# Four accumulating DMA transfers from GpSimd in place of three VectorE sums per weight block of a down projection, and PSUM banks that change roles between its two halves

## The chip, the core and the metric

The kernel runs on one core of a Trainium2 chip. A core has five engines with a program each: TensorE (PE, matrix products, with its weight loads listed apart as PEld), VectorE (DVE), ScalarE (ACT), GpSimd (POOL) and SyncE (SP, which here issues transfers). They run side by side and wait for each other by semaphores; on each engine instructions run in the order in which they are written down. The metric is device time in microseconds, the median of several executions.

## What is computed

The reference is one decoder layer for 256 tokens of width 2048. The change lies in its last matrix product.

```python
D_MODEL = 2048
D_FF = ((8 * D_MODEL // 3 + 255) // 256) * 256      # 5632
...
        x = x + rmsnorm(mix, post_mix_norm[l])

        hf = rmsnorm(x, pre_ffn_norm[l])
        ff = (jax.nn.silu(hf @ w_gate[l]) * (hf @ w_up[l])) @ w_down[l]
        x = x + rmsnorm(ff, post_ffn_norm[l])
```

`w_down` is the matrix of 5632 x 2048 that the last product reads.

## The kernel before

Every float32 weight block goes through four stations. SP loads 1 MB into one of four stage buffers (`st`, 128 partitions x 2048 values). ACT makes the float16 high part (`whi`, line 99), DVE the float16 rest (`wlo`, line 100); both write into rings of eight buffers. PE multiplies: three matmuls per product (high by high, high by low, low by high).

The down projection comes last. It has two units `u` (the left and the right 1024 output columns). A unit reads 22 blocks `i`, each 256 rows of `w_down` by 1024 columns, held in `st` as four sub-blocks of 128 rows by 512 columns. Ten of the 22 (`FAST`: 0, 2, ... 18) use a scheme with 7 products in place of 8 (21 matmuls instead of 24); it needs, beside three of the sub-blocks, four sums of sub-blocks. Blocks run in the order fast, plain, fast, plain, ...; the last three of a unit are plain and are called the tail.

For a fast block `load_pair` does this, in this order: split A (high and low parts of the first three sub-blocks, 1536 columns), the sums, in place in `st` (lines 730 to 732), split B (high and low parts of the four sums, 2048 columns). A plain block has one split of 2048 columns, called S here. The first two products of a fast block and one more use split A, the other four split B. In a regular stretch ACT and DVE therefore run B, S, A of the next fast block, then the sums on DVE, B, S, A, and so on.

PSUM has eight banks, four named `acc` and four named `tmp`. In a unit, `E` (four banks, one per half of the tokens and of the columns) and `X`, `Y`, `Z`, `Q` (four more) collect the products. When the last fast block is done, `X` to `Q` are combined by one ACT copy and four DVE operations into `fix`; the tail goes into `E`; `down_out` adds the two. Before the change `E` is always `acc` and `X` to `Q` are always `tmp`.

While the last blocks of the gate and up projections (j = 20 and 21) are still being multiplied, the first down blocks are already loaded and split; the ACT and DVE operations of `swiglu` (lines 640, 645, 99, 100) stand among these splits. A tile scheduler sets the order on each engine from the program's order.

Of the kernel before, what the change touches and what calls it, by code (L numbers as in the profile page):

```python
# [14 lines left out]
ALU = mybir.AluOpType  # L15
AX = mybir.AxisListType

P = 128
# [33 lines left out]
def hymba_layer(ctx: ExitStack, tc: tile.TileContext, x, xT, pos, inv_freq, g_pre, w_in, w_lat,  # L52
                q_norm, w_uqn, w_uqp, kv_norm, w_uk, w_uv, conv_w, conv_v, g_attn,
                w_out, g_post, g_ffn, w_gu, w_dn, g_ffo, out):
    nc = tc.nc
# [28 lines left out]
    def nm(base):  # L84
        uid[0] += 1
        return f"{base}_{uid[0]}"

    def acc_tile():
        return ps_acc.tile([P, 512], F32, tag="acc", name=nm("acc"))

    def tmp_tile():
        return ps_tmp.tile([P, 512], F32, tag="tmp", name=nm("tmp"))
# [198 lines left out]
    for j in range(4):  # L291
# [6 lines left out]
        for tb in range(NTB):  # L298
# [4 lines left out]
            u = work.tile([P, 256], F32, tag="C", name=nm("u"), bufs=2)  # L303
# [322 lines left out]
    def a_of(k, tb):  # L626
        return aT[:, k // 2, 4 * tb + k % 2, :], aT[:, k // 2, 4 * tb + 2 + k % 2, :]

    def fast_of(j):

        s = FAST.index(j)
        return ([(aT[:, j, b, :], aT[:, j, 4 + b, :]) for b in range(4)]
                + [(sT[:, s, b, :], sT[:, s, 3 + b, :]) for b in range(3)])
# [50 lines left out]
    def down_out(tb, j, ps, f):  # L684
        cs = slice(j * 512, (j + 1) * 512)
        nc.vector.tensor_tensor(f, ps, f, op=ALU.add)
        nc.scalar.activation(junk_tile(512), f, AF.Square, scale=UD, accum_out=ssd[:, tb, j : j + 1])
        if j == 3:
            final_scale(tb)
        nc.vector.scalar_tensor_tensor(ffg[:, tb, cs], f, UD, g_fo[:, cs], op0=ALU.mult, op1=ALU.mult)  # L690
# [4 lines left out]
    def partial_scale(tb):  # L695
        t = smalls()
        nc.vector.tensor_reduce(t, ssd[:, tb, 0:3], axis=AX.X, op=ALU.add)
        nc.vector.tensor_scalar(t, t, 1.0 / D, EPS, op0=ALU.mult, op1=ALU.add)
        ss_part[tb] = t
# [8 lines left out]
    def final(tb):  # L708
        r = r_fin[tb]
        cuts = (0, 640, 1280, 1792, 2048)  # L710
        for j in range(4):
            cs = slice(cuts[j], cuts[j + 1])
            xs = x_back[tb][:, cs]
            nc.vector.scalar_tensor_tensor(xs, ffg[:, tb, cs], r, xs, op0=ALU.mult, op1=ALU.add)
            (nc.sync if j % 2 == 0 else nc.scalar).dma_start(out[tb * P : (tb + 1) * P, cs], xs)

    def parts_of(st, n):
        hi = wsp.tile([P, 2048], F16, tag="whi", name=nm("whi"))
        lo = wsp.tile([P, 2048], F16, tag="wlo", name=nm("wlo"))
        split(hi[:, :n], lo[:, :n], st.rearrange("p b n -> p (b n)")[:, :n], WD_S)  # L720
        return [(hi[:, c : c + 512], lo[:, c : c + 512]) for c in range(0, n, 512)]

    def load_pair(u, i):

        st = stage.tile([P, 2048], F32, tag="stage", name=nm("st")).rearrange("p (b n) -> p b n", b=4)
        nc.sync.dma_start(st, w_dn[u, i])
        if i not in FAST:
            return parts_of(st, 2048)
        parts = parts_of(st, 1536)
        nc.vector.tensor_tensor(st[:, 0:4:3, :], st[:, 0:2, :], st[:, 3:4, :].to_broadcast([P, 2, 512]), op=ALU.add)  # L730
        nc.vector.tensor_tensor(st[:, 1, :], st[:, 0, :], st[:, 1, :], op=ALU.add)
        nc.vector.tensor_tensor(st[:, 2, :], st[:, 1, :], st[:, 2, :], op=ALU.add)
        return parts + parts_of(st, 2048)


# [2 lines left out]
    TAIL = 3  # L738
    x_back = {}
    for u in range(2):  # L740
        E = [[acc_tile(), acc_tile()], [acc_tile(), acc_tile()]]
        X, Y, Z, Q = [tmp_tile() for _ in range(4)]
        begun = set()

        def mm(ps, key, a, b, last=False):

            (ah, al), (bh, bl) = a, b
            nc.tensor.matmul(ps, ah, bh, start=key not in begun, stop=False)  # L748
            nc.tensor.matmul(ps, ah, bl, start=False, stop=False)  # L749
            nc.tensor.matmul(ps, al, bh, start=False, stop=last)  # L750
            begun.add(key)

        def plain(i, w, tb, c, last=False):

            mm(E[tb][c], (tb, c), a_of(2 * i, tb), w[0 if c == 0 else 3])
            mm(E[tb][c], (tb, c), a_of(2 * i + 1, tb), w[2 if c == 0 else 1], last)

        lasts = {f: FAST[-1] == f for f in FAST}
        for n, i in enumerate(order[:-TAIL]):
            w = load_pair(u, i)  # L760
            if i not in FAST:
                for tb in range(NTB):
                    for c in range(2):
                        plain(i, w, tb, c)
                continue
            A22, A11, A12, S1, S3, S2, S4 = fast_of(i)
            end = lasts[i]
            mm(E[0][0], (0, 0), A12, w[2])
            mm(E[0][1], (0, 1), S4, w[1])
            mm(X, "X", A11, w[0], end)  # L770
            mm(Y, "Y", S2, w[4], end)
            mm(Z, "Z", S3, w[6], end)
            mm(Q, "Q", S1, w[3], end)
            mm(E[1][0], (1, 0), A22, w[5])


        xs_ = work.tile([P, 512], F32, tag="hl", name=nm("xs"))
        nc.scalar.copy(xs_, X)
        m = work.tile([P, 512], F32, tag="ss", name=nm("m"), bufs=3)
        nc.vector.tensor_tensor(m, xs_, Y, op=ALU.subtract)  # L780
        n_ = work.tile([P, 512], F32, tag="ss", name=nm("n"), bufs=3)
        nc.vector.tensor_tensor(n_, m, Z, op=ALU.add)
        q2 = work.tile([P, 512], F32, tag="ss", name=nm("q2"), bufs=3)
        nc.vector.tensor_tensor(m, Q, m, op=ALU.subtract)
        nc.vector.tensor_tensor(q2, Q, n_, op=ALU.subtract)
        fix = [[xs_, m], [n_, q2]]
        tail = [(i, load_pair(u, i)) for i in order[-TAIL:]]
        if u == 1:
            for tb in range(NTB):
                x_back[tb] = stage.tile([P, 2048], F32, tag="stage", name=nm("xb"))  # L790
                nc.sync.dma_start(x_back[tb], x_off[:, tb, :])
        i, w = tail[0]
        for tb in range(NTB):
            for c in range(2):
                plain(i, w, tb, c)
        for tb in range(NTB):
            for c in range(2):
                for i, w in tail[1:]:
                    plain(i, w, tb, c, i == order[-1])
                down_out(tb, 2 * u + c, E[tb][c], fix[tb][c])  # L800
                if u == 1 and c == 0:
                    partial_scale(tb)
            if u == 1:
                final(tb)
# [80 lines left out]
```

## Time and profile before

| | us |
|---|---|
| median of 3 runs | 1015.67 (1015.43 to 1017.02) |
| the profiled execution | 1016.03 |
| its span in the trace | 1014.2 |
| PE busy in the span | 975.7 |
| DVE busy | 742.5 |
| ACT busy | 532.5 |
| POOL busy | 37.7 |

The span runs from the first to the last traced instruction; 1.83 us of the profiled execution lie around it. PE busy is counted from pipelined matmuls whose ends are modelled, so a full PE is one that always has a matmul in flight. The down projection fills the last 230 us of the span.

### The profile page before, as it was taken

The page shows a single profiled execution, that of the slowest core. Times are in us where ns is not written, and L with a number is a line of the kernel's source. Part 1 is how long each engine was busy: PE and PEld are TensorE (multiplying, and loading weights), DVE is VectorE, ACT ScalarE, POOL GpSimd, SP SyncE. Part 2 cuts the span into 40 slices and gives each one's busy share as a digit, 9 for nine tenths or more (in the row PEclk, how much of TensorE's full clock was granted, in tenths as well). Part 3 has the DMA queues.
Part 4 walks back from the last instruction along what each step waited for, and adds up shares of the span by engine and source line. Part 5 has one row for each costly group of instructions (what it writes and reads, how often), then busy time and mean ns, then how long its engine had stood idle before and what let it go on. Part 6 is the DMA issues. An engine that isn't in the chain of part 4 may idle for free.

```text
span 1014.2 us, 11941 instructions
## 1 busy us (share of the span) xinstructions
PE 975.7 (96%) x4652; PEld 462.3 (46%) x4652; DVE 742.5 (73%) x860; ACT 532.5 (53%) x599; POOL 37.7 (4%) x50
## 2 busy tenths in 40 slices
PE   6999997999999999999999999999999999989996
PEld 2444553774444444444444444444444444434442
DVE  6699999999868886555455555555556788888787
ACT  7796665664746564454444444454443544554551
POOL 0000000034100100000000000000000000000000
PEclk9999998999999999999999999999999999999998
DMA  9874666576546998676766776777755555635453
GB/s 348 330 256 140 223 209 196 166 241 222 201 166 170 321 303 290 218 228 201 240 217 206 222 224 223 226 218 217 234 198 166 176 189 224 235 127 222 166 186 145
DMA packets 77769, 220.37 MB, mean 217 GB/s; under 512 B 49552, under 2 KB 50192, under 8 KB 55184
## 3 DMA queue, kind: packets, MB, share of 16 engines
q1 hardware_dynamic: 76992, 218.68, 64.2%
q10 hardware_dynamic: 720, 0.93, 0.3%
q8 instruction: 36, 0.59, 0.2%
q14 instruction: 21, 0.17, 0.1%
HBM read 204.25 MB, written 4.19 MB: 206 GB/s over the span
## 4 chain that ended last, share of the span: by engine, by line
PE 64%; DVE 18%; issue 5%; ACT 5%; POOL 2%; DMA 1%; DVEq 0%; POOLq 0%; ACTq 0%; SPq 0%
PE acc L146 16%; PE acc L145 16%; PE acc L144 16%; DVE wlo L100 7%; DVE arena L277 3%; PE acc L749 3%; PE acc L750 3%; PE acc L748 3%; ACT whi L99 3%; DVE st L730 1%; PE tmp L749 1%; PE tmp L750 1%; PE tmp L748 1%; POOL sm L198 1%; DVE arena L285 1%
## 5 line engine op out<-in xcount | busy, mean ns | idle before, releaser
L100 DVE SCALAR_TENSOR_TENSOR wlo<-st,whi 128x2048 f16<-128x2048 f32 (+4 forms) x211 | 451.7, 2157 | 203.3 <-ACT whi L99 203.3
L99 ACT ACTIVATE whi<-st 128x2048 f16<-128x2048 f32 (+4 forms) x211 | 376.2, 1800 | 320.7 <-PE acc L146 176.5
L144 PE MATMUL acc<-whi,arena 128*128 128x512 f16 (+1 forms) x1084 | 410.1, 378 | 5.5 <-ACT whi L99 5.5
L145 PE MATMUL acc<-wlo,arena 128*128 128x512 f16 (+1 forms) x1084 | 410.4, 379 | 3.9 <-DVE wlo L100 3.8
L146 PE MATMUL acc<-whi,arena 128*128 128x512 f16 (+1 forms) x1084 | 409.8, 378 | 0.0
L144 PEld LDWEIGHTS <-arena 128*128 128x128 f16 x1084 | 106.7, 98 | 130.2 <-ACT arena L104 4.9
L146 PEld LDWEIGHTS <-arena 128*128 128x128 f16 x1084 | 106.7, 98 | 129.6 <-issue 6.9
L145 PEld LDWEIGHTS <-arena 128*128 128x128 f16 x1084 | 106.5, 98 | 125.2 <-issue 2.5
L748 PE MATMUL acc<-whi,arena 128*128 128x512 f16 x232 | 87.9, 379 | 0.0
L749 PE MATMUL acc<-wlo,arena 128*128 128x512 f16 x232 | 87.9, 379 | 0.0
L750 PE MATMUL acc<-whi,arena 128*128 128x512 f16 x232 | 87.9, 379 | 0.0
L277 DVE SCALAR_TENSOR_TENSOR arena<-arena 128x256 f32<-128x256 f32 x184 | 78.0, 480 | 0.0
L640 ACT ACTIVATE sg<-acc,r_f 128x256 f32<-128x256 f32 x44 | 20.7, 473 | 58.8 <-PE acc L146 58.8
L749 PEld LDWEIGHTS <-arena 128*128 128x128 f16 x272 | 26.6, 98 | 32.3 <-issue 0.3
L748 PEld LDWEIGHTS <-arena 128*128 128x128 f16 x272 | 26.6, 98 | 32.1
L750 PEld LDWEIGHTS <-arena 128*128 128x128 f16 x272 | 26.6, 98 | 32.1
L283 ACT ACTIVATE x_sb<-arena 128x256 f32<-128x256 f32 x56 | 25.2, 506 | 11.7 <-DVE arena L285 11.7
L705 POOL TENSOR_TENSOR sm<-sm,neg_half 128x1 f32<-128x1 f32 x2 | 1.1, 541 | 657.0 <-DVE sm L703 657.0
L730 DVE TENSOR_TENSOR st<-st 128x1024 f32<-128x1024 f32 x20 | 24.5, 1224 | 0.6
L153 PE MATMUL tmp<-arena,whi 128*128 128x256 f16 x80 | 21.8, 273 | 0.0
L154 PE MATMUL tmp<-arena,whi 128*128 128x256 f16 x80 | 21.8, 273 | 0.0
L155 PE MATMUL tmp<-arena,wlo 128*128 128x256 f16 x80 | 21.8, 273 | 0.0
(186 smaller groups left out, 610.1 us busy)
## 6 DMA issues: line engine op xcount, KB each, us to landing
st<-in_w_gu SPq DMA_DIRECT2D x88, 1024.0 KB, 5.0
st<-in_w_dn SPq DMA_DIRECT2D x44, 1024.0 KB, 4.9
st<-in_w_out SPq DMA_DIRECT2D x16, 1024.0 KB, 5.1
st<-in_w_in SPq DMA_DIRECT2D x14, 1024.0 KB, 9.3
st<-in_w_lat SPq DMA_DIRECT2D x12, 896.0 KB, 5.0
x_sb<-in_x SPq DMA_DIRECT2D x4, 1024.0 KB, 8.7
st<-in_w_uqn SPq DMA_DIRECT2D x4, 768.0 KB, 4.9
st<-in_w_uv SPq DMA_DIRECT2D x2, 1024.0 KB, 6.0
```

Of the source, the lines that this page charges most:

```text
L99: nc.scalar.activation(hi, src, AF.Copy, scale=scale)
L100: nc.vector.scalar_tensor_tensor(lo, src, scale, hi, op0=ALU.mult, op1=ALU.subtract)
L144: nc.tensor.matmul(p_ap, xh, wh, start=(start and k == 0), stop=False)
L145: nc.tensor.matmul(p_ap, xh, wl, start=False, stop=False)
L146: nc.tensor.matmul(p_ap, xl, wh, start=False, stop=(stop and k == wgt.kt - 1))
L153: nc.tensor.matmul(ps, wh[:, c0 : c0 + P], xh, start=(k == 0), stop=False)
L277: nc.vector.scalar_tensor_tensor(cacc[:, cb, :], upad[:, cb, k : k + S], cw[:, cb, k : k + 1], cacc[:, cb, :], op0=ALU.mult, op1=ALU.add)
L283: nc.scalar.activation(t[:, i, :], upad[:, cb, k : k + S], AF.Copy, scale=cw[:, cb, k : k + 1])
L730: nc.vector.tensor_tensor(st[:, 0:4:3, :], st[:, 0:2, :], st[:, 3:4, :].to_broadcast([P, 2, 512]), op=ALU.add)
L748: nc.tensor.matmul(ps, ah, bh, start=key not in begun, stop=False)
L749: nc.tensor.matmul(ps, ah, bl, start=False, stop=False)
L750: nc.tensor.matmul(ps, al, bh, start=False, stop=last)
```

## The change

The three DVE additions become four transfers issued by GpSimd. Each reads one sub-block of `st`, adds it to another sub-block of the same `st`, and writes it there: 128 partitions x 512 float32, 256 KB. They run in the sequence 0 += 3, 3 += 1, 1 += 0, 2 += 1, which gives the same four sums. Beside that, in unit 1 `E` takes the `tmp` banks and `X` to `Q` the `acc` banks.

```diff
         parts = parts_of(st, 1536)
-        nc.vector.tensor_tensor(st[:, 0:4:3, :], st[:, 0:2, :], st[:, 3:4, :].to_broadcast([P, 2, 512]), op=ALU.add)
-        nc.vector.tensor_tensor(st[:, 1, :], st[:, 0, :], st[:, 1, :], op=ALU.add)
-        nc.vector.tensor_tensor(st[:, 2, :], st[:, 1, :], st[:, 2, :], op=ALU.add)
+
+        for d, p in ((0, 3), (3, 1), (1, 0), (2, 1)):
+            nc.gpsimd.dma_start(st[:, d, :], st[:, p, :], accum_op=ALU.add)
         return parts + parts_of(st, 2048)
...
     for u in range(2):
-        E = [[acc_tile(), acc_tile()], [acc_tile(), acc_tile()]]
-        X, Y, Z, Q = [tmp_tile() for _ in range(4)]
+
+        mine, other = (acc_tile, tmp_tile) if u == 0 else (tmp_tile, acc_tile)
+        E = [[mine(), mine()], [mine(), mine()]]
+        X, Y, Z, Q = [other() for _ in range(4)]
```

GpSimd's order in the middle of unit 0, after the change; `st_6186` and `st_6251` are two fast blocks, a DMASW semaphore counts a transfer that GpSimd issued, a DMAHW semaphore one from SP.

```order
L732 DMA st_6186<-st_6186 128x512 [waits DMAHW7_49,DMASW7_49,DVE_49]
L732 DMA st_6186<-st_6186 128x512 [waits DMASW4_49]
L732 DMA st_6186<-st_6186 128x512 [waits DMASW5_49]
L732 DMA st_6186<-st_6186 128x512 [waits DMASW6_49]
L732 DMA st_6251<-st_6251 128x512 [waits DMAHW3_49,DMASW3_49,DVE_49]
L732 DMA st_6251<-st_6251 128x512 [waits DMASW0_49]
```

The first transfer of a block waits for DVE (split A); each of the others waits for the transfer ahead of it. In the kernel before GpSimd has nothing here.

DVE's order in the same place, before the change: split S of a plain block, split A of a fast block (`st_6247`), its sums, its split B, the next S.

```order
L100 SCALAR_TENSOR_TENSOR wlo_6220<-st_6217,whi_6219 128x2048 [waits DMAHW0_49,Activation_49]
L100 SCALAR_TENSOR_TENSOR wlo_6250<-st_6247,whi_6249 128x1536 [waits DMAHW1_49,Activation_49]
L730 TENSOR_TENSOR st_6247<-st_6247 128x2x512 [waits DVE_49]
L731 TENSOR_TENSOR st_6247<-st_6247 128x512 [waits DVE_49]
L732 TENSOR_TENSOR st_6247<-st_6247 128x512 [waits DVE_49]
L100 SCALAR_TENSOR_TENSOR wlo_6257<-st_6247,whi_6256 128x2048 [waits Activation_49]
L100 SCALAR_TENSOR_TENSOR wlo_6284<-st_6281,whi_6283 128x2048 [waits DMAHW4_49,Activation_49]
```

The same place after the change, where the fast block is `st_6251`:

```order
L100 SCALAR_TENSOR_TENSOR wlo_6224<-st_6221,whi_6223 128x2048 [waits DMAHW0_49,Activation_49]
L100 SCALAR_TENSOR_TENSOR wlo_6254<-st_6251,whi_6253 128x1536 [waits DMAHW3_49,Activation_49]
L100 SCALAR_TENSOR_TENSOR wlo_6262<-st_6251,whi_6261 128x2048 [waits DMASW2_49,DMASW1_49,DMASW3_49,DMASW0_49,Activation_49]
L100 SCALAR_TENSOR_TENSOR wlo_6289<-st_6286,whi_6288 128x2048 [waits DMAHW4_49,Activation_49]
L100 SCALAR_TENSOR_TENSOR wlo_6319<-st_6316,whi_6318 128x1536 [waits DMAHW5_49,Activation_49]
```

The sums are gone from DVE, the order of the splits is the same, and split B waits for the block's four transfers.

ACT's order there after the change: B of `st_6251`, S of the plain block, A of the next fast block `st_6316`, its B.

```order
L99 ACTIVATE whi_6261<-st_6251 128x2048 [waits DMASW1_49,DMASW0_49,DMASW2_49,DVE_49,DMASW3_49,PE_49,Activation_49]
L99 ACTIVATE whi_6288<-st_6286 128x2048 [waits DVE_49,DMAHW4_49,PE_49,Activation_49]
L99 ACTIVATE whi_6318<-st_6316 128x1536 [waits DMAHW5_49,DVE_49,PE_49]
L99 ACTIVATE whi_6326<-st_6316 128x2048 [waits DMASW5_49,DMASW6_49,DMASW4_49,DMASW7_49,DVE_49,PE_49]
```

Before the change the order of these four on ACT was the same, with a wait for DVE's sums where the DMASW semaphores stand now.

## Rows read from the trace of the kernel before

**Rows 1.** The profile's page: span, and busy time of each engine.

```profile
span 1014.2 us, 11941 instructions
PE 975.7 (96%) x4652; PEld 462.3 (46%) x4652; DVE 742.5 (73%) x860; ACT 532.5 (53%) x599; POOL 37.7 (4%) x50
```

**Rows 2.** Windows, 820 to 860 us: busy time per engine, clock, DMA share, GB/s.

```profile
820.00:860.00 40.00, 40.00 (x187) 18.20 (x186) 32.91 (x22) 18.97 (x12) 0.00 (x0) 1.00 0.50 187
```

**Rows 3.** Waits from 790 us on: who waited for whom, total, times, longest.

```profile
ACT whi L99 <- DVE st L732: 98.8, 17, 7.5
...
PE acc L748 <- DVE m L686: 3.2, 1, 3.2
...
PE tmp L749 <- DVE wlo L100: 1.1, 1, 1.1
```

**Rows 4.** Timelines of ACT and DVE, one regular period: start, duration, instruction, wait.

```profile
927.10 5.08 ACT L99 ACTIVATE whi<-st 128x2048 f16<-128x2048 f32 x3 [5.83 <-DVE st L732]
...
938.04 3.71 ACT L99 ACTIVATE whi<-st 128x2048 f16<-128x2048 f32 x2 [5.85 <-DVE st L732]
...
929.05 6.16 DVE L100 SCALAR_TENSOR_TENSOR wlo<-st,whi 128x2048 f16<-128x2048 f32 x3 [2.04 <-ACT whi L99]
935.24 1.22 DVE L730 TENSOR_TENSOR st<-st 128x1024 f32<-128x1024 f32 x1
```

**Rows 5.** Groups by line and shape, 795 to 1014 us: busy, mean ns, idle.

```profile
L100 DVE SCALAR_TENSOR_TENSOR wlo<-st,whi 128x2048 f16<-128x2048 f32 x38 | 85.3, 2288 | 33.6 <-ACT whi L99 33.6
...
L99 ACT ACTIVATE whi<-st 128x2048 f16<-128x2048 f32 x38 | 70.4, 1901 | 98.8 <-DVE st L732 98.8
```

**Rows 6.** DMA issues: count, KB each, median us from issue to landing.

```profile
st<-in_w_dn SPq DMA_DIRECT2D x44, 1024.0 KB, 4.9
...
st<-in_w_in SPq DMA_DIRECT2D x14, 1024.0 KB, 9.3
...
st<-in_w_uk SPq DMA_DIRECT2D x4, 512.0 KB, 4.3
...
out<-xb SPq DMA_DIRECT2D x2, 256.0 KB, 2.5
...
arena<-arena SPq DMA_TRANSPOSE x14, 5.7
...
gpre<-in_g_pre ACTq DMA_DIRECT2D x1, 8.0 KB, 2.1
```

**Rows 7.** Timeline of DVE where the first three fast blocks are prepared.

```profile
751.40 1.23 DVE L730 TENSOR_TENSOR st<-st 128x1024 f32<-128x1024 f32 x1
...
785.07 0.87 DVE L645 SCALAR_TENSOR_TENSOR a<-acc,r_f,sg 128x256 f32<-128x256 f32 x2
...
789.34 0.75 DVE L100 SCALAR_TENSOR_TENSOR ahl<-a,ahl 128x256 f16<-128x256 f32 x2
```

**Rows 8.** Timelines of ACT and DVE around the change of unit.

```profile
862.37 7.31 ACT L99 ACTIVATE whi<-st 128x2048 f16<-128x2048 f32 x4 [5.85 <-DVE st L732]
...
874.91 1.23 DVE L730 TENSOR_TENSOR st<-st 128x1024 f32<-128x1024 f32 x1
...
888.06 0.68 DVE L784 TENSOR_TENSOR m<-tmp,m 128x512 f32<-128x512 f32 x1
```

**Rows 9.** Timelines of ACT and PE at the end.

```profile
981.77 7.31 ACT L99 ACTIVATE whi<-st 128x2048 f16<-128x2048 f32 x4 [5.85 <-DVE st L732]
...
1000.08 0.38 PE L748 MATMUL acc<-whi,arena 128*128 128x512 f16 x1
...
1003.75 0.38 PE L750 MATMUL acc<-whi,arena 128*128 128x512 f16 x1
```

**Rows 10.** Windows of PE around a pause: length, PE busy, granted clock, DMA share, GB/s.

```profile
162.00:164.00 2.00, 1.00 (x3) 0.50 0.22 84
...
166.00:168.00 2.00, 2.00 (x9) 0.69 0.68 130
168.00:170.00 2.00, 2.00 (x11) 1.00 0.94 161
```

## The prediction

> **What bounds the kernel now.** I read the page first, for the busiest engine: PE has a matmul in flight 96% of the span [rows 1]. That is an average over stages, so the stage of the change comes next. In the window from 820 to 860 us PE is full (40.00 of 40) and DVE is second with 32.91 [rows 2]. Then the list of waits from 790 us on: PE lost only 3.2 us to a PSUM bank that DVE had not yet read, and 1.1 us to a late split [rows 3]. Its large entry is another: ACT waited 98.8 us, in 17 waits, for the last of the three sums. These waits cost no time, since ACT is not the bound, but they show where the sums stand: between split A and split B of every fast block, with ACT and DVE both behind them.
>
> So the timelines of one period are next [rows 4]. ACT starts split B of a fast block at 927.10 and the next fast block's B at 938.04: 10.94 us for a pair of one fast and one plain block. Of these, 927.10 to 935.24 (8.14 us) is B, S and the next A, which on DVE follow each other: B's `wlo` can start 1.95 us after its `whi`, and the three take 6.16 us. The rest, 935.24 to 938.04 (2.80 us), is the three sums and the handover to ACT. PE needs, for the same pair, 21 + 24 = 45 matmuls; 17 steps of matmuls took 1003.75 - 1000.08 = 3.67 us [rows 9], 0.216 us each, so 9.72 us. The split loop is thus already 1.2 us slower per pair than PE; PE stays full because the rings of eight buffers give it a lead that it eats up. Two limits stand close together: PE at 9.72 and the split loop at 10.94 us.
>
> **The change, part by part.**
>
> *The sums leave DVE.* That takes 2.80 us out of the loop's 10.94 and leaves 8.14. Whether this is worth anything depends on what stands in its place.
>
> *Four transfers take their place, one after the other.* In GpSimd's order the first waits for split A on DVE, and each of the next waits for the one ahead; ACT's and DVE's split B wait for all four. Behind B in ACT's order stand S of the plain block and A of the next fast block, so neither can be done while the transfers run, and the next chain of transfers cannot start until this A is done. Nothing overlaps: a period is 8.14 us plus four times L, where L is the time from one issue, through the landing, to GpSimd's next issue. PE, which would need 9.72 us, runs empty.
>
> *L is not in the trace*: GpSimd issues no transfer before, and none adds. From below, a plain transfer of the same 256 KB, a store at the quiet end of the program, lands in 2.5 us, and the smallest of all (8 KB) in 2.1 us [rows 6]. From above, the SBUF-to-SBUF transposes take 5.7 us. An accumulating transfer reads two 256 KB operands and writes one. Nearest in bytes read is the 512 KB load with 4.3 us, part of it spent beside other loads. In the new loop few are beside it: the two 1 MB loads of a pair (4.9 us each) are released when B and S have been read, so they overlap the first transfer or two of a chain. Against that, GpSimd must notice each landing and prepare the next transfer. I take L = 4.0 us and keep 2.5 and 5.7 as ends.
>
> The Trainium skill, page "DMA: Bandwidth & Descriptors", section "Anatomy of one DMA — SWDGE (gpsimd) path", gives about 2.0 us per transfer issued by GpSimd plus its bytes at 436 GB/s. By it L would be an estimated 2.6 us and the time 1160 us. The 2.5 us store [rows 6] is near this, but no run so far shows an adding transfer.
>
> *The sum, in the profiled execution.* The first chain can start where the first sum started, at 751.40 [rows 7]. There are 20 chains of 4L, and 19 gaps between them. Gaps 1 and 2 hold `swiglu` of j = 20 and 21 too, with 0.87 us for two DVE products and 0.75 us for two small splits [rows 7]: 8.14 + 1.62 = 9.76 us each. Gap 10, at the change of unit, holds two more plain splits: 874.91 - 862.37 = 12.54 us [rows 8]; the four DVE operations on `X` to `Q`, 0.68 us each, add 2.72: 15.26. The other 16 gaps are 8.14. Together 2 x 9.76 + 15.26 + 16 x 8.14 = 165.0 us.
>
> After the last chain: in the profile, B of the last fast block starts on ACT at 981.77 [rows 9] and the span ends at 1014.2 [rows 1], 32.4 us later. After the change PE has no backlog then, but the same work: 1.95 + 2.29 us until B's `wlo` is there [rows 5], 12 matmuls of B and 72 of the tail (84 x 0.216 = 18.1 us), and the 10.1 us from the end of the last matmul (1003.75 + 0.38) to the span's end. That is 32.4 us again. PE will have been idle before it. Where PE resumes after a long pause, from 162 us on, the granted clock is 0.50, its lower level of 1.2 GHz, and it is back at the full 2.4 GHz only in the course of the window from 166 to 168 us, after about 4 us of work [rows 10]; 4 us at half speed lose some 2.1 us.
>
> Span = 751.4 + 165.0 + 32.4 + 2.1 + 80 L = 950.9 + 80 L. With the 1.83 us around the span, and 0.36 us less because the median is that much below the profiled execution, the time is 952.4 + 80 L: with L = 4.0, **1272 us**, 25% above 1015.67.
>
> *The bank roles.* Now the 3.2 us wait of PE [rows 3] comes from the first matmuls of unit 1 into `acc` banks that `down_out` of unit 0 has yet to read. After the change `E` of unit 1 takes the `tmp` banks, which are free once `X` to `Q` are combined; it is `X` to `Q` that wait for `down_out`. I cost this at nothing: the eleventh chain, some 16 us, lies over that place, and unit 0's tail (84 matmuls, 18.1 us from 4.2 us after the tenth chain) is over before the chain's end. If the chain were not there, it would be worth up to 3.2 us.
>
> *Other queues.* SP's loads of a buffer now wait for the chain's transfers besides DVE's split B, which comes later anyway; nothing moves. A fast block's buffer is reloaded when its B is done and needed more than a period later (24 us against 4.9). GpSimd's other work in this stage, the two small powers of the final norm, comes after the last chain. What is late next, behind a chain, is B on ACT, then its `wlo` on DVE, then PE.
>
> **Rivals.**
>
> 1. *The transfers are hidden, and the kernel is faster.* The place is the split loop: if the rings and the four stage buffers let ACT and DVE prepare later blocks while a chain runs, DVE's 2.80 us per pair would be free, PE would be the only bound, and the 3.2 + 1.1 us that it lost would go: 1011 us. For it: SP, ACT and DVE all have room. Against: in ACT's and DVE's order S and the next A stand behind B. It decides only below L = (9.72 - 8.14) / 4 = 0.40 us, and time is equal to before at (1015.67 - 952.4) / 80 = 0.79 us, where the smallest landing is 2.1 us. The Trainium skill, page "DMA: Bandwidth & Descriptors", section "Rules for kernel authors", hides fixed cost by issuing early and waiting late; the order leaves no work between the issue and the wait. Chance 2%, and 1% more that gains and losses end within 0.2%, which is about what a measurement here can tell from no change.
> 2. *Quiet queues: L between 2.1 and 2.9.* For it: during most of a chain nothing else moves, as at the end of the program, where 256 KB took 2.5 us. Against: twice the reads, and a new issue each time. At 2.5 us 1152 us; at 2.9, 1184. With PE at half clock throughout, its 45 matmuls would take 19.4 us and hold a period there, which is L = 2.8 in the formula, 1176 us. Chance 16%.
> 3. *Slow additions: L above 5.7.* For it: loads in crowded queues took 9.3 us [rows 6], and what the addition itself costs no row shows. Against: at most two loads run beside a chain. At 7.5 us, midway between these rows, 1552 us. Chance 13%.
>
> **How the numbers follow.** The forecast (serial chains on the path, L from 2.9 to 5.7) has 68%. The range goes from L = 2.5 (1152 us) to L = 5.7 (1408 us): the forecast's own, plus some 12 of rival 2's 16%. Slower 97%, within 0.2% 1%, faster 2%.
>
> **What would show it.** In the changed kernel's trace: ACT's wait for the last sum becomes a wait for a transfer of `st`, about 16 us in each of 20; starts of consecutive B splits lie about 24 us apart in place of 10.94; PE is busy for about half of each period, and its clock falls below full in the chains from 790 us on; four GpSimd issues per fast block stand L apart. The gaps between chains should be 8.1 us. The prediction is wrong if S or A runs on ACT during a chain, if the transfers of a chain overlap, or if L is outside 2.5 to 5.7 us.

## The result, and the profile after

The changed kernel takes **1277.05 us** (median of 4 runs, 1276.34 to 1278.7) against 1015.57 for the kernel before in the same session: a ratio of 1.2571, with an interval of 1.2554 to 1.2588. Forecast were 1272 us, 1152 to 1408.

The page of the changed kernel: span, busy times, the granted clock in 40 slices, the software queue (packets, MB, share of the 16 DMA engines), the shares of the chain that ended last, the group of the new issues, and their landing time.

```profile
span 1276.6 us, 12100 instructions
PE 1020.8 (80%) x4652; PEld 469.8 (37%) x4652; DVE 690.5 (54%) x800; ACT 532.3 (42%) x599; POOL 106.7 (8%) x130
PEclk9999999999999999999999999876677867767778
...
q0 software_dynamic: 11520, 20.98, 9.4%
...
PE 38%; DMA 20%; DVE 16%; issue 14%; ACT 6%; POOL 3%; DVEq 0%; POOLq 0%; ACTq 0%; SPq 0%
...
L732 POOL DMA_DIRECT2D st<-st x80 | 69.0, 862 | 822.5 <-DVE wlo L100 620.2
...
st<-st POOLq DMA_DIRECT2D x80, 256.0 KB, 3.3
```

Against [rows 1], DVE lost 52.0 us of work (742.5 to 690.5, 60 instructions fewer), POOL gained 69.0 in 80 issues, and no engine is above 80% busy. The 261 us more are not work: a fifth of the chain that ended last is now DMA (1% before). The row of slices (31.9 us each; a digit 9 is 0.9 or more) places it: the clock stands at 9 in the first 25, and at 6 to 8 from 798 us on, in the down projection.

The waits from 790 us on (total, times, longest), with those of the last stage before in [rows 3]:

```profile
DVE wlo L100 <- ACT whi L99: 341.2, 19, 20.4
ACT whi L99 <- DMA st<-st: 340.4, 19, 21.5
...
POOL st L732 <- DVE wlo L100: 205.8, 18, 17.7
POOL st L732 <- DMA st<-st: 183.2, 54, 6.8
PE acc L750 <- ACT whi L99: 117.9, 10, 13.5
PE tmp L750 <- ACT whi L99: 92.6, 8, 13.6
```

ACT's wait for DVE's sums (98.8 us) has become a wait for the transfers (340.4), as forecast, and this one does cost time: PE, which lost 4.3 us to others here before, waits 210.5 us for split B. The rest is the ring that follows from it: DVE waits for ACT, GpSimd for DVE and for its own transfers.

The timelines of GpSimd and ACT over one chain and the start of the next (start, duration, instruction, idle time before):

```profile
853.32 0.85 POOL L732 DMA_DIRECT2D st<-st  x1 [10.94 <-DVE wlo L100]
858.46 0.87 POOL L732 DMA_DIRECT2D st<-st  x1 [4.29 <-DMA st<-st]
862.06 0.85 POOL L732 DMA_DIRECT2D st<-st  x1 [2.73 <-DMA st<-st]
865.61 0.87 POOL L732 DMA_DIRECT2D st<-st  x1 [2.70 <-DMA st<-st]
877.40 0.85 POOL L732 DMA_DIRECT2D st<-st  x1 [10.92 <-DVE wlo L100]
...
868.99 5.08 ACT L99 ACTIVATE whi<-st 128x2048 f16<-128x2048 f32 x3 [19.00 <-DMA st<-st]
893.09 5.08 ACT L99 ACTIVATE whi<-st 128x2048 f16<-128x2048 f32 x3 [19.02 <-DMA st<-st]
```

Read from top to bottom: an issue, the wait for its landing, the next issue, four times, 5.14, 3.60, 3.55 and 3.38 us apart; at 868.99 ACT starts B, S and A as one group. The next chain starts 8.41 us after that. A period is 868.99 to 893.09, 24.10 us, against 10.94 in [rows 4].

What lies between the chains shows in the chain of work that ended last, at the same place (start, duration, what):

```profile
870.97 1.78 issue
...
873.14 3.96 DVE wlo L100 x2
877.11 0.29 issue
877.40 4.91 DMA st<-st
882.31 0.28 issue
882.59 3.25 DMA st<-st
```

DVE ends split A at 877.10 and GpSimd issues at 877.40; each landing is followed by 0.28 us before the next issue.

Windows in a regular stretch and over most of unit 1 (busy times with instructions of PE, PEld, DVE, ACT, POOL; clock; DMA share; GB/s):

```profile
860.00:900.00 40.00, 16.85 (x59) 6.44 (x59) 11.13 (x6) 10.17 (x6) 5.16 (x6) 0.66 0.44 109
1060.00:1240.00 180.00, 86.69 (x328) 34.45 (x327) 43.13 (x21) 36.16 (x22) 25.90 (x31) 0.73 0.47 126
```

PE is busy for 48% of the second window, at a mean clock of 0.73, between its two levels of 1.2 and 2.4 GHz; in [rows 2] it was full at 1.00. DMA moves less than before (109 GB/s against 187).

Taken together over all 20 chains, from first issue to the start of B on ACT, and the 19 gaps between:

| | forecast | measured |
|---|---|---|
| start of the first chain | 751.4 | 751.08 |
| 20 chains | 320.0 (L = 4.0) | 321.7 (L = 4.02) |
| 19 gaps | 165.0 | 170.5 |
| after the last chain | 34.5 | 33.3 |
| span | 1270.9 | 1276.6 |

### The profile page after: what moved, and what is told of

Read it like the earlier page. It is cut to its first block, busy times and chain, and to the rows that moved or that the text cites. A ratio compares the mean times of both kernels' runs of the same rounds, so it can differ in the third digit from the quotient of the medians.

```text
span 1276.6 us, 12100 instructions
## 1 busy us (share of the span) xinstructions
PE 1020.8 (80%) x4652; PEld 469.8 (37%) x4652; DVE 690.5 (54%) x800; ACT 532.3 (42%) x599; POOL 106.7 (8%) x130
## 4 chain that ended last, share of the span: by engine, by line
PE 38%; DMA 20%; DVE 16%; issue 14%; ACT 6%; POOL 3%; DVEq 0%; POOLq 0%; ACTq 0%; SPq 0%
DMA st<-st 19%; PE acc L146 12%; PE acc L145 12%; PE acc L144 12%; DVE wlo L100 9%; ACT whi L99 4%; DVE arena L277 2%; POOL st L732 1%; POOL sm L198 1%; DVE arena L285 1%; POOL ss L469 1%; POOL arena L488 0%; DMA st<-in_w_uqn 0%; DVE xb L714 0%; DMA st<-in_w_lat 0%
## 5 line engine op out<-in xcount | busy, mean ns | idle before, releaser
L144 PEld LDWEIGHTS <-arena 128*128 128x128 f16 x1084 | 106.7, 98 | 130.6 <-ACT arena L104 5.0
L146 PEld LDWEIGHTS <-arena 128*128 128x128 f16 x1084 | 106.7, 98 | 129.3 <-issue 6.6
L145 PEld LDWEIGHTS <-arena 128*128 128x128 f16 x1084 | 106.4, 98 | 125.0 <-issue 2.3
L732 POOL DMA_DIRECT2D st<-st x80 | 69.0, 862 | 822.5 <-DVE wlo L100 620.2
L750 PE MATMUL acc<-whi,x_sb 128*128 128x512 f16 x30 | 13.9, 531 | 117.9 <-ACT whi L99 117.9
L750 PE MATMUL tmp<-whi,x_sb 128*128 128x512 f16 x30 | 13.6, 501 | 92.6 <-ACT whi L99 92.6
L750 PEld LDWEIGHTS <-x_sb 128*128 128x128 f16 x60 | 6.0, 101 | 216.3 <-issue 211.3
L750 PE MATMUL acc<-whi,arena 128*128 128x512 f16 x136 | 57.6, 427 | 9.5 <-DVE a L645 9.5
L750 PE MATMUL tmp<-whi,arena 128*128 128x512 f16 x136 | 57.6, 431 | 0.0
L751 PE MATMUL acc<-wlo,arena 128*128 128x512 f16 x136 | 54.1, 398 | 0.0
L752 PE MATMUL acc<-whi,arena 128*128 128x512 f16 x136 | 53.7, 395 | 0.0
L751 PE MATMUL tmp<-wlo,arena 128*128 128x512 f16 x136 | 53.4, 393 | 0.1
L752 PE MATMUL tmp<-whi,arena 128*128 128x512 f16 x136 | 52.8, 388 | 0.0
L751 PEld LDWEIGHTS <-arena 128*128 128x128 f16 x272 | 28.0, 103 | 46.8 <-issue 18.4
L750 PEld LDWEIGHTS <-arena 128*128 128x128 f16 x272 | 29.5, 108 | 41.7 <-issue 16.7
```

The source lines that it names most:

```text
L144: nc.tensor.matmul(p_ap, xh, wh, start=(start and k == 0), stop=False)
L145: nc.tensor.matmul(p_ap, xh, wl, start=False, stop=False)
L146: nc.tensor.matmul(p_ap, xl, wh, start=False, stop=(stop and k == wgt.kt - 1))
L732: nc.gpsimd.dma_start(st[:, d, :], st[:, p, :], accum_op=ALU.add)
```

## The experiments

The first experiments set the theory (serial chains on the path) against the rivals that were left: PE at a lower clock as the bound, a cost per byte or per transfer, and the bank roles. The kernel before ran beside them, with medians between 1015.94 and 1016.17 us; each ratio is to the one that ran beside that experiment.

**1 and 2. Each half alone.** First the bank roles with the three sums on DVE, then the transfers with the banks of before (all diffs are against the changed kernel):

```diff
-        for d, p in ((0, 3), (3, 1), (1, 0), (2, 1)):
-            nc.gpsimd.dma_start(st[:, d, :], st[:, p, :], accum_op=ALU.add)
+        nc.vector.tensor_tensor(st[:, 0:4:3, :], st[:, 0:2, :], st[:, 3:4, :].to_broadcast([P, 2, 512]), op=ALU.add)
+        nc.vector.tensor_tensor(st[:, 1, :], st[:, 0, :], st[:, 1, :], op=ALU.add)
+        nc.vector.tensor_tensor(st[:, 2, :], st[:, 1, :], st[:, 2, :], op=ALU.add)
```

```diff
-        mine, other = (acc_tile, tmp_tile) if u == 0 else (tmp_tile, acc_tile)
-        E = [[mine(), mine()], [mine(), mine()]]
-        X, Y, Z, Q = [other() for _ in range(4)]
+        E = [[acc_tile(), acc_tile()], [acc_tile(), acc_tile()]]
+        X, Y, Z, Q = [tmp_tile() for _ in range(4)]
```

Expected of the banks alone:

> The bank roles alone, with the three sums on VectorE. If the whole loss is the chain of transfers, this is no slower than the kernel before: 1012 to 1016 us, and at best 3.2 us faster, the wait of PE for a bank at the change of unit that goes. If the bank roles carry part of the loss (the rival), it is above 1020 us.

Expected of the transfers alone:

> The four transfers alone, with the bank roles of before. Chain theory: the bank roles are hidden under the eleventh chain, so the time is that of the changed kernel, 1274 to 1280 us. If the bank roles save or cost something beside the chains, it differs from 1277 by 5 us or more.

The transfers alone: 1278.17 us, ratio 1.2583 (1.2564 to 1.2603), chains 320.1 and gaps 170.5. They are the whole change. The banks alone: 1018.25 us over 11 runs, ratio 1.0021 (1.0013 to 1.003), so 2.1 us slower, where a gain or nothing had been expected. Its waits of PE from 780 us on, and its windows at the change of unit:

```profile
PE acc L751 <- DVE n L686: 2.6, 1, 2.6
...
PE acc L751 <- DVE m L686: 1.9, 1, 1.9
```

```profile
880.00:905.00 25.00, 20.47 (x87) 8.85 (x86) 23.89 (x24) 10.84 (x15) 0.00 (x0) 0.93 0.45 168
895.00:900.00 5.00, 2.14 (x7) 0.78 (x7) 5.00 (x7) 3.36 (x7) 0.00 (x0) 0.90 0.87 298
900.00:905.00 5.00, 5.00 (x19) 2.09 (x18) 4.69 (x5) 0.30 (x3) 0.00 (x0) 0.76 0.30 125
```

The same stretch of the kernel before, and two rows of PE's timeline in experiment 1 that are nine matmuls apart:

```profile
880.00:905.00 25.00, 21.77 (x101) 9.76 (x100) 24.10 (x24) 11.13 (x14) 0.00 (x0) 1.00 0.44 168
```

```profile
898.88 0.54 PE L752 MATMUL acc<-wlo,x_sb 128*128 128x512 f16 x1
...
902.51 0.38 PE L752 MATMUL tmp<-wlo,arena 128*128 128x512 f16 x1
```

PE waits once more for DVE to empty a bank, now 4.5 us in two pieces (3.2 in [rows 3]), since it is now `X` to `Q` that take the banks of `down_out`. But the wait of 1.1 us for a late split in [rows 3] is gone, so all waits together are 4.5 us against 4.3. What is new is the clock: from 895 on it falls to 0.90 and then 0.76, where the kernel before has 1.00 (0.93 against 1.00 over the whole stretch, with PE busy for 20.47 and 21.77 us). The nine matmuls take 3.63 us, where nine at the full clock take 1.94 (0.216 us each). In this execution the lower clock thus costs 1.7 us and the waits 0.2, close to the 2.1 measured. The two profiled executions lie 1.24 us apart (1017.27 and 1016.03), in part because this one came into the stage 0.4 us ahead. The seven executions of experiment 1 with 1018.25 us or more have a mean clock of 0.988, the profiled one 0.991; that the same stretch is longer in them is likely, but no trace of them shows it. My step "if the chain were not there, it would be worth up to 3.2 us" is wrong in sign.

**3. Two transfers, two sums.** The first two of the sequence stay transfers, the last two go back to DVE.

```diff
-        for d, p in ((0, 3), (3, 1), (1, 0), (2, 1)):
+        for d, p in ((0, 3), (3, 1)):
             nc.gpsimd.dma_start(st[:, d, :], st[:, p, :], accum_op=ALU.add)
+        nc.vector.tensor_tensor(st[:, 1, :], st[:, 0, :], st[:, 1, :], op=ALU.add)
+        nc.vector.tensor_tensor(st[:, 2, :], st[:, 1, :], st[:, 2, :], op=ALU.add)
```

> The first two sums by transfers, the last two by VectorE (0.72 us each); the result is the same. Chain theory: each block loses two steps of 3.53 us and gains 1.5 us, so 20 x 5.5 = 110 us less, 1167 us (1155 to 1180). If the slower clock of PE is what bounds the periods, a pair holds at 45 matmuls of 0.43 us, 19.4 us, and PE shows no idle time in the loop.

1163.91 us, ratio 1.1449 (1.1432 to 1.1467), as expected. The time goes with the number of transfers in a row. PE is busy for only 25.15 of the 40 us from 860 on, so its clock does not hold the period.

**4. A quarter of the columns.** Each transfer adds 128 of the 512 columns; the sums of the other 384 are left out.

```diff
-            nc.gpsimd.dma_start(st[:, d, :], st[:, p, :], accum_op=ALU.add)
+            nc.gpsimd.dma_start(st[:, d, 0:128], st[:, p, 0:128], accum_op=ALU.add)
```

> The same four transfers with 128 of 512 columns each, 64 KB for 256 KB; three quarters of each sum are left out. If a step is mostly a fixed time from issue to landing, steps fall from 3.53 to about 2.9 us and the time to about 1230 us (1210 to 1250). If a step goes by its bytes, the part beyond the 0.86 us that GpSimd is busy falls to a quarter, steps are near 1.5 us, and the time is about 1115 us.

1198.2 us, ratio 1.1797 (1.1779 to 1.1814): a miss, between the two cases and outside the range of the first. Its timeline of GpSimd over one chain:

```profile
876.62 0.85 POOL L732 DMA_DIRECT2D st<-st  x1 [9.99 <-DVE wlo L100]
881.41 0.87 POOL L732 DMA_DIRECT2D st<-st  x1 [3.94 <-DMA st<-st]
884.08 0.85 POOL L732 DMA_DIRECT2D st<-st  x1 [1.79 <-DMA st<-st]
886.70 0.87 POOL L732 DMA_DIRECT2D st<-st  x1 [1.77 <-DMA st<-st]
```

The first row starts the chain; the issues take the same 0.85 to 0.87 us as with 256 KB, and the steps behind the second and third are 2.67 and 2.62 us. Over all chains a step other than the first takes 2.58 us with 64 KB, and 3.53 with 256 KB. The 192 KB make 0.95 us, so, on a straight line through these two sizes, 0.32 us per 64 KB (about 205 GB/s of result) and a fixed part of 2.58 - 0.32 = 2.26 us, 64% of a step of 256 KB.

The Trainium skill, page "DMA: Bandwidth & Descriptors", section "Anatomy of one DMA — SWDGE (gpsimd) path", has the same form: about 2.0 us and bytes at 436 GB/s. The fixed part agrees within 0.3 us (2.26 measured); the bytes of an adding transfer took 1.27 us for 256 KB, against an estimated 0.60 by the page, so about twice.

**5. Light loads.** SP loads 256 KB per block in place of 1 MB; GpSimd fills the other three sub-blocks with a constant, so the weights of these are left out. The chain itself is unchanged.

```diff
-        nc.sync.dma_start(st, w_dn[u, i])
+        nc.gpsimd.memset(st[:, 1:4, :], 0.5)
+        nc.sync.dma_start(st[:, 0:1, :], w_dn[u, i][:, 0:1, :])
```

> The changed kernel, but each down block loads only its first sub-block (256 KB for 1 MB); GpSimd fills the other three with a constant between the chains, so the product is not the reference's. If the first transfer of a chain (5.49 us against 3.53 for the others) is slow because two loads run beside it, it falls to 3.6 to 3.9 us and the time by 20 x 1.7 = 34 us, to 1243 us (1235 to 1252). If the first is slow for a reason of its own (a first issue after a wait for VectorE), nothing moves, 1277 us.

1241.35 us, ratio 1.2218 (1.22 to 1.2236). Chains fall from 321.7 to 286.5 us: the first transfer takes 3.80 us in the mean in place of 5.49, the other three 3.51 in place of 3.53. What is long in the first transfer is thus the loads beside it; two of 1 MB are released by B and S just before it.

**6. Fewer matmuls.** The third matmul of each product of the down projection is left out.

```diff
             nc.tensor.matmul(ps, ah, bh, start=key not in begun, stop=False)
-            nc.tensor.matmul(ps, ah, bl, start=False, stop=False)
-            nc.tensor.matmul(ps, al, bh, start=False, stop=last)
+            nc.tensor.matmul(ps, ah, bl, start=False, stop=last)
```

> The changed kernel without the third matmul of each product in the down projection, so a third of PE's work there is left out. If the chains set the period, only PE's work behind the last chain counts: 84 matmuls become 56, 6 us less, 1271 us (1267 to 1274). If PE at its lower clock sets the period (the rival), a third of the 257 us that PE is busy there goes, some 85 us, to 1190 us.

1273.99 us, ratio 1.2535 (1.2512 to 1.2557). A third less work for PE in this stage gives 3 us: neither PE nor its clock bounds the changed kernel. The 3 us themselves are a sum of several changes: in the traces the time after the last chain falls from 33.3 to 29.7 us and the chains from 321.7 to 315.0, but gap 10 grows from 15.2 to 20.7, because DVE there does all of `down_out` of unit 0 ahead of split A.

**7. Split B one period later.** `load_pair` is cut into a load of a fast block (load, A, transfers) and one of a plain block, and the loop runs S, the next A, and only then B of the block whose transfers were issued a period ago.

```diff
+        cur = load_fast(u, fasts[0])
+        for k, i in enumerate(fasts):
+            wp = load_plain(u, plains[k]) if k < len(plains) else None
+            nxt = load_fast(u, fasts[k + 1]) if k + 1 < len(fasts) else None
+            st, w = cur
+            w = w + parts_of(st, 2048)
+            cur = nxt
```

> The same transfers, but the program asks for split S of the plain block and split A of the next fast block before split B, so that ACT and DVE work while a chain runs and the next chain waits only for the one ahead on GpSimd. Chain theory: the gaps of 8.4 us vanish and the period is one chain, 15 to 16 us; 20 chains in a row and the ends give about 1105 us (1085 to 1130). If the period is set by something else (PE's clock, or the DMA engines' share), it stays near 24 us and the time near 1277 us.

1132.84 us, ratio 1.1146 (1.1129 to 1.1163), just above what was expected. The timeline of GpSimd, where x2 are two issues side by side, the last of one chain and the first of the next:

```profile
851.39 1.75 POOL L729 DMA_DIRECT2D st<-st  x2 [7.27 <-DMA st<-st]
856.52 0.87 POOL L729 DMA_DIRECT2D st<-st  x1 [3.38 <-DMA st<-st]
860.13 0.85 POOL L729 DMA_DIRECT2D st<-st  x1 [2.75 <-DMA st<-st]
868.99 1.75 POOL L729 DMA_DIRECT2D st<-st  x2 [8.01 <-DMA st<-st]
```

The gaps are gone, so B, S and A are hidden, and a period is 868.99 - 851.39 = 17.60 us. But now both loads of a pair start in the chain, at 859.05 and 861.25, and the transfer issued at 860.13 takes until 868.99, 8.86 us. The chain alone is longer than PE's 9.72 us.

**8. Only S moved into the chain** (order A, S, B), with the same two functions:

```diff
+        for k, i in enumerate(fasts):
+            st, w = load_fast(u, i)
+            wp = load_plain(u, plains[k]) if k < len(plains) else None
+            w = w + parts_of(st, 2048)
```

> The same transfers, with only split S of the plain block moved into the chain (order A, S, B). Chain theory: the gap loses one split of 2.2 us on VectorE in each period, 20 x 2.2 = 44 us less, 1233 us (1225 to 1243). If the order of the splits does not matter, 1277 us.

1260.48 us, ratio 1.2394 (1.2356 to 1.2433): a miss by 27 us. The gaps did what was said (6.20 us each, 128.2 in all, 42.3 less), but the chains rose from 321.7 to 344.2. One chain of it:

```profile
872.99 0.85 POOL L729 DMA_DIRECT2D st<-st  x1 [8.76 <-DVE wlo L100]
877.35 0.87 POOL L729 DMA_DIRECT2D st<-st  x1 [3.51 <-DMA st<-st]
883.15 0.85 POOL L729 DMA_DIRECT2D st<-st  x1 [4.93 <-DMA st<-st]
886.71 0.87 POOL L729 DMA_DIRECT2D st<-st  x1 [2.71 <-DMA st<-st]
```

The second step is 5.80 us in place of 3.6. S, read early, frees its stage buffer early, and SP starts the next load there at 874.91, inside the chain. The new theory, that half the gain was given back to contention, was tried by itself.

**9. The same with light loads.** Order A, S, B with the edit of experiment 5; three of four sub-blocks are a constant again.

> The transfers with split S inside the chain (the order A, S, B that ran at 1260 us where 1233 were expected), and each down block loads only its first sub-block, the others are filled with a constant by GpSimd, so the product is not the reference's. If the 22 us were given back because loads run beside the chains, steps return to 3.5 us and chains to 14.1: 20 x 14.1 plus gaps of 128 us give 1196 us (1186 to 1206). If the splits of ACT and VectorE beside the chain slow the transfers, chains stay at 17.2 us and the time is near 1258 us.

1202.72 us, ratio 1.1839 (1.1819 to 1.1859), as expected. Steps are 3.70 us for the first and 3.61 for the rest, chains 290.9, gaps 128.2. With light loads the order takes 1241.35 - 1202.72 = 38.6 us off (experiment 5); with full loads only 16.6.

The Trainium skill, page "DMA: Bandwidth & Descriptors", section "Issuing engines are not separate DMA queues", says that transfers share the DMA engines whichever engine issues them. SP's loads and GpSimd's transfers agree with it here: the same adding transfer took 3.5 us alone and up to 8.86 beside two loads.

**10 to 12. What PE's wait at the change of unit is.** After experiment 1 I took the order in which banks are given out for the cause. Experiment 10 keeps the sums on DVE and gives unit 1 the banks in the order in which they come free; 11 keeps the banks of before and puts S between the sums and B, so that ACT has S to do while DVE adds; 12 is both. The program's order in 11 is A, sums, S, B; the expectation recorded for it, below, has S ahead of the sums, which is not what the edit does. The diffs are unit 1 of experiment 10 and the load of experiment 11, whose loop is that of experiment 8.

```diff
+            e00, e01, X, Y = [tmp_tile() for _ in range(4)]
+            Z, Q, e10, e11 = [acc_tile() for _ in range(4)]
```

```diff
+    def load_fast(u, i):
...
         parts = parts_of(st, 1536)
+        nc.vector.tensor_tensor(st[:, 0:4:3, :], st[:, 0:2, :], st[:, 3:4, :].to_broadcast([P, 2, 512]), op=ALU.add)
...
+        return st, parts
```

> No transfers; sums on VectorE as before. In unit 1 the four products that come first (two of E, X and Y) take the tmp banks, which are free early, and the other four the acc banks, in the order in which down_out of unit 0 frees them. If the 2 us that the changed bank roles cost by themselves come from the third to fifth product meeting acc banks that are not yet read, PE's waits at the change of unit (3.2 us before) go: 1011 to 1014 us. If the roles do not matter there, 1015 to 1017 us.

> No transfers, bank roles of before; only the order of the splits is A, S, sums, B, so that ACT works while VectorE adds. The split loop falls from 10.94 to about 8.9 us, under PE's 9.72. PE waits for a split only 1.1 us in the kernel before, so the time is 1014 to 1016 us. If the sums on VectorE had bounded the kernel, as the change supposes, it would fall by 10 us or more.

> Both of the last two together, without any transfer. PE's 3.2 and 1.1 us of waiting go: 1011 to 1013 us. If the waits only move elsewhere, 1015 to 1017 us.

Experiment 10: 1016.26 us over 11 runs, ratio 1.0004 (0.9995 to 1.0013), no change, a miss. Its waits of PE:

```profile
PE acc L753 <- DVE n L686: 2.6, 1, 2.6
PE tmp L754 <- DVE wlo L100: 1.1, 1, 1.1
PE acc L753 <- DVE m L686: 0.7, 1, 0.7
```

4.4 us, where [rows 3] have 4.3: other banks, the same late DVE. Experiment 11: **1010.89 us**, ratio 0.9951 (0.9939 to 0.9964), 5.3 us faster than before and better than expected; 12: 1011.74, ratio 0.9955 (0.9942 to 0.9967), within the interval of 11. In 11 PE has no wait at all from 780 us on. Its window at the change of unit, and DVE's timeline in unit 0:

```profile
880.00:905.00 25.00, 25.00 (x118) 11.33 (x117) 21.59 (x22) 12.29 (x14) 0.00 (x0) 1.00 0.40 144
```

```profile
821.37 1.22 DVE L728 TENSOR_TENSOR st<-st 128x1024 f32<-128x1024 f32 x1
...
824.89 6.16 DVE L100 SCALAR_TENSOR_TENSOR wlo<-st,whi 128x2048 f16<-128x2048 f32 x3 [0.84 <-ACT whi L99]
831.09 1.23 DVE L728 TENSOR_TENSOR st<-st 128x1024 f32<-128x1024 f32 x1
```

ACT's timeline at the same place:

```profile
822.95 3.90 ACT L99 ACTIVATE whi<-st 128x2048 f16<-128x2048 f32 x2 [3.65 <-PE acc L753]
```

PE is full where it had 21.77 of 25 us before; the waits of 4.3 us in [rows 3], which are gone, are most of the 5.3 gained. The period is 831.09 - 821.37 = 9.72 us, which is the estimate of PE's own need, against 10.94 in [rows 4]: DVE waits 0.84 us for ACT in place of 2.04, since ACT starts S at 822.95, while DVE, from 821.37 on, still adds; these 1.20 us are nearly the whole gain of a period. What ACT waits for before S is PE, for a free buffer (29.7 us in 14 waits from 780 us on), so the splits run ahead as far as the rings allow. In unit 1 ACT's order of the splits is B, A, S, and the period is 10.82 us (919.54 to 930.36 for the first sums); why the scheduler chose it there was not tried.

## Why the prediction was right, point by point

**What bounded the kernel before.** PE and the split loop close together, as forecast: in experiment 11 the loop runs at 9.72 us, PE's own pace, and the whole gain is 5.3 us.

**Serial chains on the path.** Shown. Experiment 2 gives the whole time with the transfers alone, 3 some half of it with half the transfers ((1163.91 - 1016) / (1277.05 - 1016) = 57%), and 6 leaves the time with a third of PE's work gone. That is against the part of rival 2 in which PE at half clock holds the period. Rival 1 (hidden) would have needed L under 0.40 us.

**L = 4.0.** The mean was 4.02, but of two kinds: 5.49 us for the first of a chain and 3.53 for the other three. The argument had both parts (two loads beside the first transfer, 512 KB read), but they were not forecast apart, and that their sizes came out at one round number is luck. Experiment 4 gives 2.26 us fixed and 1.27 for the bytes, and experiment 5 that 1.7 of the 1.96 us more in the first transfer come from the loads beside it. Rival 3 (slow additions) was wrong about the addition, yet its other half, crowding, is what experiments 7 and 8 ran into.

**Gaps of 8.14.** The term that was mis-sized: regular gaps were 8.40, the two of `swiglu` 10.09 (9.76 forecast), gap 10 15.2 (15.26). I took the handover from split A to the next issue at that of DVE to itself (929.05 + 6.16 to 935.24 in [rows 4], 0.03 us); from DVE to GpSimd it is 0.29. Over the 19 gaps these 0.26 us make 4.9 of the 5.5 us; most of the rest is one gap of 9.07 us, whose first issue came 0.96 us after DVE's end in place of 0.29, for no reason that the trace shows. The gaps are nearly all of the difference: -0.3 at the start, +1.7 in the chains, +5.5 in the gaps, -1.2 at the end make 5.7 us = 1276.6 - 1270.9.

**What PE does.** Right in kind: 48% busy at a clock of 0.73, and 33.3 us after the last chain against 34.5. One reading in that last term was wrong: PE starts as soon as B's `whi` is there, 1.95 us after B's start, and not after the 2.29 us of `wlo` that the sum adds.

```profile
1245.25 1.01 PE L750 MATMUL acc<-whi,x_sb 128*128 128x512 f16 x2 [13.46 <-ACT whi L99]
```

The matmuls from here on, at a granted clock of 0.50 until 1249 us, take 2.6 us longer than at the full one (2.1 forecast); with a longer stretch behind the last matmul (10.4 us, 10.1 forecast) this gives back nearly half. ACT's waits were 17.9 us each (340.4 / 19) where I said about 16: it also waits out what is left of split A on DVE, which lies in the gap, so the sum is not touched.

**The bank roles at nothing.** Right inside this change (1277.05 with them and 1278.17 without, intervals that overlap), but the side sentence on their worth alone was wrong: they cost 2.1 us, most of it at the lower clock. The wait that I read as a bank held by `down_out` is DVE being late with it: with other banks (10) it moves, with DVE relieved (11) it is gone. Why the clock falls after this pause in experiment 1, and not in the profiled executions of experiment 10 and of the kernel before, is open; other executions may differ (one of experiment 10 took 1019.23 us at a mean clock of 0.987, the profiled one 1015.54 at 0.991).

## What to carry to other kernels

Before work is moved from an engine with slack to a transfer, count how many transfers come one after the other and what is queued behind the wait: twenty chains of four transfers cost 261 us here, where all the DVE work that they replaced was 52 us. Hiding a chain behind other work gains less where that work releases loads onto the same DMA engines: the order with light loads gave 38.6 us, with full ones 16.6. And where one engine waits for another's short step in every period, put a piece of other work between the two in program order: this alone, with nothing moved to another engine, gave 0.5%.

## What the runs showed of the hardware that was not expected

- An adding transfer of 128 x 512 float32 inside SBUF took 3.53 us from its issue to the step behind it, and one of 128 x 128 took 2.58: on a straight line 2.26 us fixed and 0.32 us per 64 KB, with GpSimd busy for 0.86 us at each issue whether it moves 64 or 256 KB.
- One such transfer took 3.5 us alone, 5.49 in the mean with the end of two 1 MB loads beside it, and 8.86 in experiment 7 with both starting beside it.
- In the profiled executions, PE's waits of 1.9 and 2.6 us, three matmuls apart (experiment 1), were followed by 5 us at a mean clock of 0.76; those of 0.7 and 2.6 (experiment 10) and of 3.2 (the kernel before) were not.
